# Order of the input products in the second block's mixer, with its tables and norm sums moved

## The chip, the cores and the metric

One core of a Trainium2 chip runs the whole program in one launch. The metric is the device time of an execution in microseconds (us); the kernel before took 3211.77 us (median of 3 runs, 3209.35 to 3212.21). TensorE (PE) does the matrix products and its weight loads (PEld), VectorE (DVE), ScalarE (ACT) and GpSimd (POOL) the elementwise work; SyncE (SP) and POOL issue the transfers.

## The reference

Three residual layers on x of 256 tokens by 2048 features. The first block has two (attention, then a gated linear recurrence, each with a swiglu). The second block, which the change touches, is:

```python
ada = silu(c) @ w_ada + b_ada                      # sh_m, sc_m, gt_m, sh_f, sc_f, gt_f
h = rmsnorm(x, g_pre_mix) * (1 + sc_m) + sh_m
proj = h @ w_in                                    # q (16 heads of 64), k, v (2 heads), u (1024)
attn = sliding_window_attention(q, k, v, sinks)    # window 128, softmax with a sink
y = s5_ssm(u, ...)                                 # complex diagonal state space, 64 groups of 16
z = gelu(y);  ssm = z * sigmoid(z @ w_glu)
merged = concat(rmsnorm(attn, g_attn), rmsnorm(ssm, g_ssm))
x = x + (1 + gt_m) * rmsnorm(merged @ w_out, g_post_mix)
h = rmsnorm(x, g_pre_ffn) * (1 + sc_f) + sh_f
up = causal_conv(h @ w_up);  x = x + (1 + gt_f) * rmsnorm((gelu(gate) * val) @ w_down, g_post_ffn)
```

## The kernel before

Every large product runs in three parts of split float32: the weight tile and the activations are each a high and a low part (`wh`, `wl`; two halves of `hx`), and high*high, high*low and low*high are added in PSUM. A weight tile (512 KB, tile `wr`) is loaded by SP, cast to `wh` by ACT (line 278) and subtracted to `wl` by DVE (line 97), up to two tiles ahead of its use. `gemm` and `gemm_t` walk the list of weight tiles that `plan_weights` has written; after each tile they call `tick()`, which moves every spawned generator (a "task") on to its next `yield`. So a task's yields say after how many weight tiles its next piece is traced.

That traced order is not the order on the chip. When the kernel is built, a planner puts the instructions of each engine in order by its own estimates of their durations, the traced order being the priority; weight splits and some evacuations carry a higher one (`high_priority(offset=200)`). Tiles come from pools: 56 slots of 2 KB per partition ("s"), 2 double PSUM banks for the large products (`pg`), and 4 single PSUM banks ("pa") that all small products share. On each engine the planned order is then fixed, and an instruction that isn't ready holds those behind it.

The second block's mixer (`mixer2`, from line 1232) begins at about 2123 us of the trace. Its input product `w_in` has nine column blocks of 256: block 4 with 5 (k, v and the first four query heads), 6 to 8 (the other query heads), 0 to 3 (u). Before, they run as 4, 6, 7, 8, 0, 1, 2, 3, each four weight tiles. Each query block spawns two `swa` tasks (line 1351): after two yields one head each tick (scores `psc`, softmax with Exp), later the transposes `pst`, then the values `pso`, the copies `at`, `ac` and a sum of squares. Each u block calls `utask`, which evacuates u and makes a copy `u4` by sixteen 32-partition copies on ACT (line 1245), and spawns an `ssm` task (line 1250): after one yield 32 narrow products `psz` (64 columns), then a rotation on DVE and POOL, two scans, a second rotation, and for each half the products `psy`, a Gelu (`zf`) and its split `zc`. Exp and Gelu are in different activation tables; `act` (line 115) traces a table load where the function isn't in the set that is loaded, and ties the activations of a set behind its load and the next load behind them.

An `ssm` task needs seven slots of tables (`rC`, `rS`, `rD`, four `bt`), which POOL's queue loads with 19 transfers from DRAM, where an earlier task wrote them. Before, all four sets are traced right behind the block 4 product.

After the input products come the attention half of the output product (`out2a`, four column blocks j), the four `glu` products, and the state-space half (`out2b`). `stat_rs` sums squares over the partitions by 12 products of 2 columns (`psn`) and turns the sum into 1/rms on DVE; for the state-space norm it is run by `rs_task`, two ticks into `out2b`. The rows that scale the next normalization (`d_gpf`, `d_ggf`) are made by `make_row` (line 1204: a transpose `psw`, a copy on ACT, a store by POOL), before `mixer2` begins.

Of the kernel before, what the change touches and what calls it, by code (L numbers as in the profile page):

```python
# [44 lines left out]
def ktiles(k0, k1, nkt=NKT):  # L45
    n = k1 - k0
    cnt = -(-n // nkt)
    out, a = [], k0
    for i in range(cnt):
        b = k0 + (n * (i + 1) + cnt - 1) // cnt  # L50
        out.append((a, b))
        a = b
    return out


class Build:
# [120 lines left out]

    LOAD_AHEAD, SPLIT_AHEAD, KEPT = 4, 2, 4

    def plan_weights(self):  # L180
        A = self.A
        S = []

        def add(key, aps, k0, k1, width=256, kept=0):
            seq = []
            tiles = ktiles(k0, k1, 1024 // width)
            K = []
            for i, (a, b) in enumerate(tiles):
                for bi, ap in enumerate(aps):
                    e = (ap[:, a:b, :], b - a, width, i >= len(tiles) - kept)  # L190
                    (K if e[3] else S).append(e)
                    seq.append((bi, a, b))

            for i, e in enumerate(K):
                S.insert(len(S) - 2 * (len(K) - i) + 1, e)
            self.plan.append((key, len(aps), seq))

        def out_gemm(key, w, k0, k1, kept=0):
            for j in range(4):
                add((key, j), [w[j]], k0, k1, 512, kept if j == 3 else 0)  # L200

        def ffn(l):
            for h in range(2):
                for b in self.FFN_BLOCKS[h]:
                    add(("g", l, b), [A[f"wg{l}"][b]], 0, 16, 512)
                    add(("u", l, b), [A[f"wu{l}"][b]], 0, 16, 512)
                out_gemm(("d", l, h), A[f"wd{l}"], 24 * h, (24, 44)[h], self.KEPT if l and h else 0)

        self.plan = []
        for b in (0, 1, 2, 3, 5, 4):  # L210
            add(("qkv", b), [A["wqkv"][b]], 0, 16, 512)

        seq = [(bi, a, a + 2) for r in (range(0, 12, 2), range(12, 16, 2)) for bi in range(2) for a in r]
        S.extend((A["wo"][bi][:, a:b, :], 2, 512, False) for bi, a, b in seq)
        self.plan.append((("wo", 0), 2, seq))
        for j in (2, 3):
            add(("wo", j), [A["wo"][j]], 0, 16, 512)
        ffn(0)
        for n in range(8):
            add(("xb", n), [A["wrin"][n]], 0, 16)  # L220
        for o, i in self.RNN_ORDER:
            if o == "g":
                add(("gt", i), [A["wgt"][i]], 0, 8)
            elif o == "y":
                add(("yb", i), [A["wrin"][8 + i]], 0, 16)
        out_gemm("wrout", A["wrout"], 0, 16)
        ffn(1)
        add(("in2", 4), [A["win2"][4], A["win2"][5]], 0, 16)
        for b in (6, 7, 8, 0, 1, 2, 3):
            add(("in2", b), [A["win2"][b]], 0, 16)  # L230
        out_gemm("out2a", A["wout2"], 0, 8)
        for b in range(4):
            add(("glu", b), [A["wglu"][b]], 0, 8)
        out_gemm("out2b", A["wout2"], 8, 16, self.KEPT)
        first = True
        for h in range(2):
            for b in range(11 * h, 11 * h + 11):
                if first:
                    add(("ug2", b), [A["wup2"][b], A["wup2"][22 + b]], 0, 16)
                    first = False  # L240
                else:
                    add(("u2", b), [A["wup2"][b]], 0, 16)
                    add(("g2", b), [A["wup2"][22 + b]], 0, 16)
            out_gemm(("d2", h), A["wdn2"], 22 * h, 22 * h + 22, self.KEPT if h else 0)
        self.S = S
        self.wt, self.kept = {}, []
        self.n_load = self.n_split = self.n_use = 0
        self.split_on = ["av"]
# [978 lines left out]
        self.stt(o, self.ada[:, 16 * i:16 * i + 16], 1.0, self.vec(g), ADD, MUL)  # L1227
        return o

    def mixer2(self, hx, first, rest, d_gg, d_gp):  # L1230
        nc = self.nc
        u, u4 = [None] * 4, [None] * 4

        def utask(n, ps):
            t = self.slot("ut")
            nc.scalar.copy(out=t, in_=ps[:, :, 256:512])
            o = u[n] = self.slot("u", (128, 2, 4, 64))
            for m in range(2):
                v = "p (k i) -> p i k"
                self.tt(o[:, m], ps[:, m, 0:256].rearrange(v, i=4), t[:, m, :].rearrange(v, i=4), ADD)  # L1240

            w = u4[n] = self.slot("u4", (128, 2, 4, 64))
            for lag in range(4):
                for g in range(4):
                    nc.scalar.copy(out=w[32 * lag:32 * lag + 32, :, g, :], in_=o[32 * g:32 * g + 32, :, lag, :])
# [3 lines left out]

        def ssm(q):  # L1250
            R, bt = tabs[q]
            yield
            C, S, D0 = R
            a, b, c, d = (self.slot(n, (128, 8, 64)) for n in "abcd")
            psz = [self.bank("psz").rearrange("p (j k) -> p j k", j=8) for _ in range(2)]
# [60 lines left out]
        self.spawn(rest(), False)  # L1316
        ps, psq = self.gemm(("in2", 4), hx)
        tabs = []
        for q in range(4):
            R = [self.slot(n, (128, 8, 64)) for n in ("rC", "rS", "rD")]  # L1320
            for i in range(3):
                nc.gpsimd.dma_start(out=R[i].rearrange("p a b -> p (a b)"),
                                    in_=self.d_rt[i, :, 512 * q:512 * q + 512])
            bt = {}
            for i in range(2):
                t = [self.slot("bt", (128, 4, 128)) for _ in range(2)]
                for cc in range(2):
                    bt[cc, i] = t[cc]
                    for lag in range(4):
                        nc.gpsimd.dma_start(out=t[cc][32 * lag:32 * lag + 32], in_=self.d_bt[i, lag, :, 2 * q + cc, :]  # L1330
                                            .rearrange("(g r) n -> r g n", g=4))
            tabs.append((R, bt))
        kv = self.evac(ps, "kv")
        k2, v2 = kv[:, 0, :], kv[:, 1, :]
        VP = []
# [70 lines left out]
            yield  # L1406

        ats = []
        for b in range(4):
            if b:  # L1410
                psq, = self.gemm(("in2", 5 + b), hx)
            q = self.evac(psq, "q2")
            for m in range(2):
                ats.append(self.spawn(swa(2 * b + m, q[:, m, :])))
        sts = []
        for n in range(4):
            ps, = self.gemm(("in2", n), hx)
            utask(n, ps)
            sts.append(self.spawn(ssm(n)))
        self.finish(vt, *ats)  # L1420
        self.stat_rs(sta)

# [1 line left out]
        for j in range(4):  # L1424
            ps = self.gemm_t(("out2a", j), ac)
# [22 lines left out]
        for b in range(4):  # L1448
            ps, = self.gemm(("glu", b), zc)
# [11 lines left out]
        hx = [None] * 16  # L1461
        scaled, first, rest = self.modulated(st, rows, self.ada[:, 48:64], hx)
# [8 lines left out]
            scaled(0, t)  # L1471

        def rs_task():
            yield
            yield
            self.stat_rs(sts_)

        strs = self.spawn(rs_task())
        for j in range(3):
            ps = self.gemm_t(("out2b", j), sc, 8)  # L1480
# [2 lines left out]
            for t in range(2):  # L1483
                one(j, t, ps[:, t, :])
        self.gemm_t(("out2b", 3), sc, 8, half)
        return hx, first, rest

    def post(self, mix, st, t, st2=None):

# [77 lines left out]
    def main(self):  # L1567
# [50 lines left out]
        d_ggm = self.make_row("d_ggm", self.gated("gg_m", "g_post_mix", 2))  # L1618
        self.pace = 0.45
        ada = self.spawn(self.paced(self.ada_task(72, 96)), False)  # L1620
        ssm = self.spawn(self.ssm_task())
        st2 = self.tstat()
        rows = {}
        hx = [None] * 16
        scaled, first, rest = self.modulated(st2, rows, self.ada[:, 0:16], hx)
# [9 lines left out]

        self.ffn(1, xc, st, strs, None, st2, None, half)
        self.finish(ssm, ada)
        d_gpf = self.make_row("d_gpf", self.gated("gp_f", "g_pre_ffn", 4))
        d_ggf = self.make_row("d_ggf", self.gated("gg_f", "g_post_ffn", 5))
        hx, first, rest = self.mixer2(hx, first, rest, d_ggm, d_gpf)  # L1640
        self.ffn2(hx, first, rest, d_ggf)


# [120 lines left out]
```

## Time and profile before

| | |
|---|---|
| median of 3 runs | 3211.77 us |
| the profiled execution | 3212.04 us, span of its instructions 3210.3 us |
| granted TensorE clock, mean | 0.988 of full |
| PE busy | 3128.8 us, 97% of the span |
| DVE, ACT, POOL busy | 2210.5, 1588.5, 543.9 us |
| HBM | 218 GB/s over the span |

Busy time is the union of an engine's instructions. A wait is idle time of an engine ahead of an instruction, put down to what released it. The granted clock of a stretch is 1.00 at 2.4 GHz and 0.50 at 1.2 GHz.

### The profile page before, as it was taken

Reading aid. Unit: us, or ns where it says so; the run is one execution under the profiler, and the core shown is the slowest. Engines: PE = TensorE matmul, PEld = TensorE weight load, DVE = VectorE, ACT = ScalarE, POOL = GpSimd, SP = SyncE. Lnnn points to the kernel's source line nnn. Section 1 sums busy time; section 2 is a strip of 40 time slices with the busy share of each in tenths; the row PEclk is TensorE's granted clock in tenths of the full one; section 3 lists DMA queues with packets and bytes.
Section 4 is the critical chain, followed back from the end, with each engine's and each line's share of the span. In section 5 each row is a group of like instructions: output and inputs, shape, how many; then the busy total and the mean of one; then the engine's idle time right before and its main releaser. Section 6 shows DMA issues by size and latency. Waiting matters only on the chain. (4 is left out here: it accounts for less than half of the span.)

```text
span 3210.3 us, 43992 instructions
## 1 busy us (share of the span) xinstructions
PE 3128.8 (97%) x16104; PEld 2632.9 (82%) x16104; DVE 2210.5 (69%) x3336; ACT 1588.5 (49%) x2294; POOL 543.9 (17%) x755
## 2 busy tenths in 40 slices
PE   8999999999999989999999999999998999999998
PEld 6888888888888878788887888878886888888887
DVE  7766777767777899666676667556657766456665
ACT  5554444344444477544443444447455555445553
POOL 1000000000000043087352624232211000000000
PEclk9999999999999999999999999999898999999999
DMA  7447888988887644677777777675454555655564
GB/s 264 138 142 240 283 279 282 314 269 281 278 279 263 235 145 156 189 247 253 248 258 238 241 245 247 214 220 149 141 173 148 189 188 189 196 189 188 201 192 163
DMA packets 232009, 702.54 MB, mean 219 GB/s; under 512 B 27248, under 2 KB 35504, under 8 KB 231536
## 3 DMA queue, kind: packets, MB, share of 16 engines
q1 hardware_dynamic: 221136, 671.11, 64.1%
q0 software_dynamic: 9936, 27.57, 2.7%
q8 instruction: 126, 2.06, 0.3%
q10 hardware_dynamic: 720, 1.06, 0.1%
q14 instruction: 91, 0.75, 0.1%
HBM read 683.86 MB, written 15.76 MB: 218 GB/s over the span
## 5 line engine op out<-in xcount | busy, mean ns | idle before, releaser
L97 DVE TENSOR_TENSOR wl<-wr,wh 128x1024 fp32r<-128x1024 f32 x1072 | 1352.7, 1266 | 725.9 <-ACT wh L278 646.3
L278 ACT CAST wh<-wr 128x1024 fp32r<-128x1024 f32 x1028 | 1081.6, 1052 | 1377.3 <-PE pg L143 1161.5
L143 PE MATMUL pg<-wh,xc 128*128 128x512 f32 x3200 | 802.6, 392 | 7.4 <-ACT wh L278 7.4
L143 PEld LDWEIGHTS pg<-wh,xc 128*128 128x128 f32 x3200 | 597.7, 188 | 129.8 <-ACT wh L278 7.4
L143 PE MATMUL pg<-wh,hc 128*128 128x512 f32 x2200 | 548.7, 391 | 0.0
L143 PEld LDWEIGHTS pg<-wh,hc 128*128 128x128 f32 x2200 | 410.3, 188 | 84.2
L143 PE MATMUL pg<-hh,wh 128*128 128x512 f32 x1696 | 431.3, 395 | 2.1 <-DVE kv L97 2.1
L143 PE MATMUL pg<-wl,xc 128*128 128x512 f32 x1600 | 430.1, 390 | 1.5 <-DVE wl L97 1.5
L956 DVE SCALAR_TENSOR_TENSOR aw<-aw,cb 128x512 f32<-128x512 f32 x384 | 280.9, 745 | 109.0 <-DMA aw<-in_wada 103.5
L143 PEld LDWEIGHTS pg<-hh,wh 128*128 128x128 f32 x1696 | 306.1, 190 | 60.1 <-issue 4.6
L143 PEld LDWEIGHTS pg<-wl,xc 128*128 128x128 f32 x1600 | 300.3, 188 | 64.6 <-DVE wl L97 2.4
L143 PE MATMUL pg<-wl,hc 128*128 128x512 f32 x1100 | 295.5, 390 | 5.5 <-DVE wl L97 5.4
L143 PEld LDWEIGHTS pg<-wl,hc 128*128 128x128 f32 x1100 | 205.8, 188 | 50.2 <-DVE wl L97 7.6
L143 PEld LDWEIGHTS pg<-hh,wl 128*128 128x128 f32 x1696 | 231.3, 190 | 16.8 <-issue 0.3
L143 PE MATMUL pg<-hh,wl 128*128 128x256 f32 x1696 | 237.7, 283 | 0.0
L97 POOL TENSOR_TENSOR i<-i,xv 128x512 f32<-128x512 f32 x16 | 30.3, 1895 | 962.5 <-ACT i L124 962.5
L143 PE MATMUL pg<-xc,wh 128*128 128x512 f32 x512 | 128.9, 394 | 6.0 <-DVE wh L284 5.0
L143 PEld LDWEIGHTS pg<-xc,wh 128*128 128x128 f32 x512 | 92.1, 189 | 23.6 <-DVE wh L284 5.8
L1219 POOL DMA_DIRECT2D row<-d_ggf x4 | 2.2, 547 | 566.0 <-PE pg L143 542.7
L143 PEld LDWEIGHTS pg<-xc,wl 128*128 128x128 f32 x512 | 69.8, 192 | 13.4 <-DVE wl L97 9.2
L143 PE MATMUL pg<-xc,wl 128*128 128x256 f32 x512 | 73.1, 286 | 5.6 <-DVE wl L97 5.5
L106 DVE SCALAR_TENSOR_TENSOR cv<-xpad,vecs,cv 128x256 f32<-128x256 f32 x176 | 73.4, 479 | 0.0
(328 smaller groups left out, 2831.7 us busy)
## 6 DMA issues: line engine op xcount, KB each, us to landing
aw<-in_wada SPq DMA_DIRECT2D x384, 256.0 KB, 4.7
wr<-in_wg SPq DMA_DIRECT2D x176, 512.0 KB, 4.0
wr<-in_wu SPq DMA_DIRECT2D x176, 512.0 KB, 4.0
wr<-in_wd SPq DMA_DIRECT2D x176, 512.0 KB, 4.5
wr<-in_wup SPq DMA_DIRECT2D x176, 512.0 KB, 4.7
wr<-in_wdn SPq DMA_DIRECT2D x88, 512.0 KB, 3.6
wr<-in_wrin SPq DMA_DIRECT2D x64, 512.0 KB, 4.7
wr<-in_wqkv SPq DMA_DIRECT2D x47, 512.0 KB, 3.5
```

The costliest lines, as they stand in the source:

```text
L97: return (eng or self.nc.vector).tensor_tensor(out=out, in0=a, in1=b, op=op)
L106: return self.nc.vector.scalar_tensor_tensor(out=out, in0=a, scalar=s, in1=b, op0=op0, op1=op1)
L143: self.nc.tensor.matmul(out, lhsT, rhs, start=start, stop=stop, **kw)
L278: c = self.nc.scalar.copy(out=wh[:, :n, :], in_=wr[:, :n, :])
L956: nc.vector.scalar_tensor_tensor(out=t, in0=t, scalar=1.0, in1=cb[i % 4], op0=MUL, op1=MUL, accum_out=part[:, i // 4, i % 4:i % 4 + 1])
L1219: self.nc.gpsimd.dma_start(out=t, in_=d[4 * j:4 * j + 4, :].rearrange("(o a) b -> o (a b)", o=1) .to_broadcast([128, 512]))
```

## The change

The query blocks and the u blocks are taken in turn (6, 0, 7, 1, 8, 2, 3), in the list of weight tiles and in `mixer2`. Each set of state-space tables is traced by a function `tables(q)` at four places: 0 behind the block 4 product, 1 and 2 behind query blocks 6 and 7, 3 behind u block 1. An `ssm` task yields twice, not once, ahead of `psz`. The two `make_row` calls for the norm rows move from before `mixer2` to behind `tables(0)`. `rs_task` yields four times, not twice.

```diff
+    IN2_ORDER = (6, 0, 7, 1, 8, 2, 3)
...
-        for b in (6, 7, 8, 0, 1, 2, 3):
+        for b in self.IN2_ORDER:
             add(("in2", b), [A["win2"][b]], 0, 16)
...
-    def mixer2(self, hx, first, rest, d_gg, d_gp):
+    def mixer2(self, hx, first, rest, d_gg):
...
         def ssm(q):
             R, bt = tabs[q]
-            yield
+            for _ in range(2):
+                yield
             C, S, D0 = R
...
         tabs = []
-        for q in range(4):
+
+        def tables(q):
             R = [self.slot(n, (128, 8, 64)) for n in ("rC", "rS", "rD")]
...
             tabs.append((R, bt))
+
+        tables(0)
+        d_gp = self.make_row("d_gpf", self.gated("gp_f", "g_pre_ffn", 4))
+        d_ggf = self.make_row("d_ggf", self.gated("gg_f", "g_post_ffn", 5))
...
         ats = []
-        for b in range(4):
-            if b:
-                psq, = self.gemm(("in2", 5 + b), hx)
-            q = self.evac(psq, "q2")
+        sts = []
+
+        def heads(b, ps):
+            q = self.evac(ps, "q2")
             for m in range(2):
                 ats.append(self.spawn(swa(2 * b + m, q[:, m, :])))
-        sts = []
-        for n in range(4):
-            ps, = self.gemm(("in2", n), hx)
-            utask(n, ps)
-            sts.append(self.spawn(ssm(n)))
+
+        heads(0, psq)
+        for b in self.IN2_ORDER:
+            ps, = self.gemm(("in2", b), hx)
+            if b > 4:
+                heads(b - 5, ps)
+                if b < 8:
+                    tables(b - 5)
+                continue
+            utask(b, ps)
+            sts.append(self.spawn(ssm(b)))
+            if b == 1:
+                tables(3)
         self.finish(vt, *ats)
         self.stat_rs(sta)
...
         def rs_task():
-            yield
-            yield
+            for _ in range(4):
+                yield
             self.stat_rs(sts_)
...
-        d_gpf = self.make_row("d_gpf", self.gated("gp_f", "g_pre_ffn", 4))
-        d_ggf = self.make_row("d_ggf", self.gated("gg_f", "g_post_ffn", 5))
-        hx, first, rest = self.mixer2(hx, first, rest, d_ggm, d_gpf)
+        hx, first, rest, d_ggf = self.mixer2(hx, first, rest, d_ggm)
         self.ffn2(hx, first, rest, d_ggf)
```

## Rows read from the trace of the kernel before

**Rows 1.** The page's head and first part: busy us, share, instructions of an engine.
```profile
span 3210.3 us, 43992 instructions
PE 3128.8 (97%) x16104; PEld 2632.9 (82%) x16104; DVE 2210.5 (69%) x3336; ACT 1588.5 (49%) x2294; POOL 543.9 (17%) x755
```

**Rows 2.** Waits of PE, whole span: us in total, times, longest us.
```profile
...
PE psz L143 <- ACT u L1245: 3.0, 3, 2.0
PE psn L143 <- ACT sq L120: 2.3, 1, 2.3
PE pg L143 <- DVE kv L97: 2.1, 1, 2.1
PE psz L143 <- ACT sPT L1389: 1.5, 1, 1.5
...
```

**Rows 3.** Windows: length, busy us (instructions) by engine, granted clock, DMA share, GB/s.
```profile
...
2156.78:2188.45 31.67, 29.53 (x167) 24.74 (x167) 20.12 (x59) 17.61 (x44) 18.75 (x35) 1.00 0.94 252
...
2245.31:2256.77 11.46, 11.46 (x49) 10.71 (x50) 5.66 (x7) 3.38 (x7) 2.53 (x2) 0.55 0.15 46
...
2272.19:2283.55 11.36, 11.36 (x105) 11.00 (x105) 5.96 (x7) 0.85 (x3) 2.49 (x2) 0.70 0.23 72
...
2308.30:2330.34 22.04, 21.22 (x214) 18.90 (x214) 16.88 (x29) 9.62 (x24) 5.28 (x5) 1.00 0.61 189
...
2410.41:2425.00 14.59, 14.59 (x56) 12.25 (x57) 10.58 (x23) 8.29 (x15) 1.98 (x1) 0.78 0.57 187
...
```

**Rows 4.** Timeline of PE: start, us, engine, line, operation, out<-in, count, idle before.
```profile
...
2158.92 2.06 PE L143 MATMUL pg<-hh,wh 128*128 128x512 f32 x8 [2.14 <-DVE kv L97]
...
2245.31 6.28 PE L143 MATMUL psz<-u,bt 128*128 128x64 f32 x32 [1.47 <-ACT sPT L1389]
...
2272.19 6.07 PE L143 MATMUL psz<-u,bt 128*128 128x64 f32 x32 [1.95 <-ACT u L1245]
...
2295.06 1.71 PE L143 MATMUL psz<-u,bt 128*128 128x64 f32 x12 [0.21 <-ACT u L1245]
...
2320.21 3.98 PE L143 MATMUL psz<-u,bt 128*128 128x64 f32 x32 [0.82 <-ACT u L1245]
...
```

**Rows 5.** Timeline of ACT ahead of the first `psz` and behind it.
```profile
...
2243.84 0.91 ACT L1245 COPY u<-u 32x128 f32<-32x128 f32 x3
...
2244.77 1.24 ACT L1389 COPY sPT<-pst 128x384 f32<-128x384 f32 x3
...
2246.04 1.28 ACT L135 ACT_TABLE_LOAD   x1
2247.33 0.48 ACT L1389 COPY sPT<-pst 128x384 f32<-128x384 f32 x1
...
```

**Rows 6.** Groups of ACT's instructions, 2120 to 2430: count, busy us, mean ns.
```profile
...
L1245 ACT COPY u<-u 32x128 f32<-32x128 f32 x64 | 18.9, 296 | 5.6 <-DVE u L97 4.7
...
```

**Rows 7.** Timeline of all engines around the state-space norm's sums.
```profile
...
2406.98 1.17 PE L143 MATMUL pg<-wh,sc 128*128 128x512 f32 x4
...
2409.69 1.13 ACT L120 ACTIVATE sq<-gl 128x256 f32<-128x256 f32 x2
...
2410.41 0.59 PE L143 MATMUL psn<-ones,sq 128*128 128x2 f32 x2 [2.25 <-ACT sq L120]
2410.62 1.21 ACT L120 ACTIVATE sc<-gl,vecs 128x256 fp32r<-128x256 f32 x2
...
2411.36 1.27 DVE L106 SCALAR_TENSOR_TENSOR sc<-gl,vecs,sc 128x256 fp32r<-128x256 f32 x2 [0.32 <-ACT sc L120]
...
```

**Rows 8.** Timeline of PE at the mixer's beginning.
```profile
...
2124.87 0.28 PE L1207 MATMUL psw<-ct,gg_f 128*16 128x128 f32 x1 [0.23 <-DVE xt L97]
...
2128.50 1.09 PE L1187 MATMUL psx<-ct,y 128*128 128x128 f32 x4 [3.35 <-DVE y L106]
...
```

**Rows 9.** Timeline of POOL: the first and the last of its table transfers.
```profile
...
2127.18 0.58 POOL L1322 DMA_DIRECT2D rC<-d_rt  x1
...
2190.50 0.55 POOL L1330 DMA_DIRECT2D bt<-d_bt  x1 [0.35 <-DMA bt<-d_bt]
...
```

More of the change, by code (lines that the diff above doesn't have):

```diff
@@ L1485, in mixer2 @@
         self.gemm_t(("out2b", 3), sc, 8, half)
-        return hx, first, rest
+        return hx, first, rest, d_ggf
     def post(self, mix, st, t, st2=None):
```

## The prediction, as put on record

> **What bounds the kernel now.** Read the page's head first: PE works 3128.8 of 3210.3 us, DVE 69%, ACT 49% [rows 1]. The products themselves aren't changed, so the kernel can only win what PE loses: idle time, and time at the lower of its two clocks. The second view is PE's waits. Those that the change can reach are small: three on the `u` copies, 3.0 us, one on an `sPT` copy, 1.5 us, and one on the norm's squares, 2.3 us; the 2.1 us on `kv` stands at a place that the change leaves as it is [rows 2]. The third view is the granted clock by windows, and it shows a loss that no list of waits has: behind the first `psz` group PE has 0.55, behind the second 0.70, behind the late norm sums 0.78, and 1.00 in the stretches beside them [rows 3]. 1.00 is 2.4 GHz and 0.50 is 1.2 GHz, so a window's length times what it lacks to 1.00 is the loss: 11.46 x 0.45 = 5.2 us, 11.36 x 0.30 = 3.4 us, 14.59 x 0.22 = 3.2 us. The fourth view, PE's timeline, shows what went before. A wait of 1.47 and one of 1.95 us ahead of 32 narrow products were followed by the low clock; waits of 0.21 and 0.82 us ahead of the same products were not, nor was 2.14 us ahead of full-width ones [rows 4].
>
> So at stake are, for the four `psz` groups, 1.47 + 5.2 + 1.95 + 3.4 + 0.21 + 0.82 = 13.0 us, and for the norm sums 2.25 + 3.2 = 5.4 us [rows 3, 4, 7]: 18.4 us, 0.6% of the span. Nothing else that is slow lies in reach.
>
> **Part 1, the order.** No instruction is added to PE, DVE or POOL; what moves is when they come due. Counting yields: before, the first `psz` is traced in the tick of the last heads' transposes `pst`, and its wait ends on the copy `sPT` of such a transpose, which sits on ACT right behind the last three `u4` copies [rows 4, 5]. The four "pa" banks explain that: `psz` takes two, one still held by a `pst`. After, with two yields, the `psz` of u blocks 0, 1, 2 fall in ticks 10, 18, 26 behind the block 4 product, where the running heads trace nothing (scores in ticks 6, 7, 14, 15, 22, 23, transposes in 9, 17, 25, values in 11, 19, 27). That clash goes.
>
> What is late next is ACT. Sixteen copies at 0.296 us are 4.7 us [rows 6], and casts come between; the second to fourth `psz` all waited for them, by 1.95, 0.21 and 0.82 us [rows 2, 4], though the planner had put other products first. Its estimate is short, and the extra yield doesn't mend that, since a `psz` that isn't ready by plan is planned later anyway. Three of four copy chains now run beside softmaxes. The price per `psz` lies between 0.21 us (third) and 1.47 + 5.2 = 6.6 us (first). I take one of the four at 6.0 us, the mean of the two that lost the clock, and three at 0.5 us, the mean of the two that didn't: 7.5 us, a gain of 13.0 - 7.5 = 5.5 us. The ends are four at 0.21 (gain 12.2) and four at 6.6 (loss 13.4).
>
> **Part 2, activation tables.** Before, all Exp of the heads come ahead of all Gelu of the state space, and one load of 1.28 us lies between [rows 5]. After, by the same count of yields, Gelu falls in ticks 15, 18, 23, 26 and Exp in 14, 15, 22, 23: the set changes seven times, six more, 6 x 1.28 = 7.7 us of ACT. ACT is busy 17.6 of 31.7 us with heads in flight [rows 3], so most of that hides in its idle time; the load in tick 18 stands inside the copy chain of u block 1 (spawned at tick 16). I charge one load, 1.3 us; ends 0 and 7.7 us. The ties between sets also force an order: the second Exp of query block 2 behind the first Gelu of u block 0, which waits for its `psy`. By the traced order that `psy` lies seven ticks behind its u block, and nothing but the heads' own later steps waits for that Exp, so I give it no price of its own.
>
> **Part 3, tables as needed.** The same 76 transfers. Before they ran on POOL from 2127.2 to 2191.1 us [rows 9] beside full DMA traffic (share 0.94) with PE at clock 1.00 and no PE wait on a transfer [rows 2, 3]. Spread out they can collide with POOL's two products of each rotation, which come behind them on its queue: 64 us for four sets is 16 us each. Sets 1, 2 and 3 are traced in ticks 4, 12 and 16 and read by `psz` in ticks 18, 26 and 30; 14 ticks of more than 2 us each [rows 4] cover 16 us, so the data is in time, and slots are free for longer. I take 0; ends -1 us (a slot comes sooner) and +4 us (a rotation behind transfers, cover gone).
>
> **Part 4, norm rows.** Two transposes `psw` go from an idle stretch of 3.35 us on PE [rows 8], where they cost nothing, to the first product. There they take 2 x 0.28 = 0.6 us unless they fall in the `kv` wait [rows 4]. Their two copies on ACT and two stores on POOL are small and wait for nothing. The row that ends the 3.35 us is DVE's `y`, so removing them does not shorten it. I take +0.3 us; ends 0 and 0.6.
>
> **Part 5, norm sums later.** `psn` now stands behind the fourth weight tile of `out2b`, not the second, so PE doesn't meet the late square. But the fourth tile needs the `sc` made of the same `glu` output. From 2406.98 us, the third tile's 12 products at about 0.25 us [rows 4] end near 2409.9; the first high half of `sc` is there at 2410.62 + 0.6 = 2411.2, its low half at 2411.36 + 0.64 = 2412.0 [rows 7]. PE waits 1.3 + 0.6 = about 2 us, as long as before: the wait changes its name. What can be won is the clock, because full-width products follow now instead of 2-column ones; the 2.14 us ahead of full-width products kept it [rows 4]. Half of 3.2: gain 1.6 us. Ends: 3.2, and -2 us if the norm's DVE chain, now shorter by two tiles of cover, holds up the bank that column block 2 needs.
>
> **Sum.** 5.5 - 1.3 - 0 - 0.3 + 1.6 = 5.5 us faster. The profiled execution took 3212.04 us, 1.7 us more than its span and 0.3 us over the median: 3212.0 - 5.5 = 3206.5, and by the median 3206.3. I forecast **3206 us**.
>
> **Rivals.** (A) Every wait becomes as short as the fourth `psz` (0.82 us) and the clock holds throughout: 13.0 - 4 x 0.82 = 9.7, plus 3.2, plus nothing lost to tables: 12.9 us, **3199 us**. For it: the bank clash goes and narrow groups lie among wide products; against it: two of three waits on the copies weren't due to the clash. (B) The losses move and stay: the two expensive `psz` lose 6 us again under other names and the norm's wait goes to `sc` with the low clock behind it: **3211 us**. For it speaks that an ACT behind its plan caused most waits; against it that one cause of two at `psz` is gone. (C) Slower: the loads of activation tables decide. Those in ticks 18 and 26 stand in the copy chains of u blocks 1 and 2 and push them from 1.7 us (mean of the two long waits) to 1.7 + 1.28 = 3.0 us, beyond the length from which the low clock followed (1.47 us; 0.82 us didn't); each then costs 3.0 + 4.3 = 7.3 us. With the first at 6.6 and the last at 0.8 that is 22.0 against 13.0, and 0.3 for the transposes: +9.3 us, **3221 us**. For it: six loads certain; against: ACT has 14 us idle in 31.7 [rows 3]. The Trainium skill speaks for it too: "ScalarE: Activation LUTs", section "Table sets: the hidden batching unit" wants functions grouped by set, and its section "What ACT_TABLE_LOAD costs" puts a switch at about 2.66 us with the drain. The trace bears out only the load: 1.28 us, the next copy 0.01 us behind it [rows 5]; by the page six switches would be an estimated 16 us of ACT. That the change doesn't do what it says is possible for part 3 (the planner may issue the transfers as soon as slots are free, as now); the time is then the forecast's.
>
> **Numbers.** 0.2%, 6.4 us, is about what a measurement can tell from no change: below 3205.3 is faster, above 3218.2 slower. Forecast 0.44, with its own range of 3201 to 3211, half of it below 3205.3; A 0.20; B 0.22; C 0.14. Faster 0.22 + 0.20 = 0.42, same 0.22 + 0.22 = 0.44, slower 0.14. The range takes in A and most of the way to C: 3196 to 3220.
>
> **What would show it.** Right: seven table loads among heads and state space; `psz` waits on `u` copies, not on `sPT`; at most one or two windows under 0.9 between 2160 and 2330 us; no wait at `psn`, but one of some 2 us on `sc` ahead of the fourth `out2b` tile; the `psw` in the first product and PE's 3.35 us wait unchanged. Wrong: waits on `psy` or scans behind POOL's transfers, a wait of the second `out2b` pair for a `pg` bank, or a low clock behind three or four `psz`.

## The result, and the profile after

The changed kernel takes 3237.74 us (median of 4 runs, 3233.33 to 3244.71) where the kernel before takes 3211.99 beside it: 1.0082 of its time (95% interval 1.0070 to 1.0094), 26 us slower. The forecast was 3206, the range ended at 3220.

The profiled execution took 3241.56 us. Its page begins with the rows that answer to [rows 1]:

```profile
span 3239.8 us, 43999 instructions
PE 3134.5 (97%) x16104; PEld 2635.6 (81%) x16104; DVE 2212.0 (68%) x3336; ACT 1596.2 (49%) x2300; POOL 544.2 (17%) x755
```

The counts of instructions are the same but for six more on ACT, the activation table loads. Where the time went is read from windows by stage: the input product, the attention half of the output product (`out2a`) and the state-space half (`out2b`). Before:

```profile
core 0: us, PE busy (x) PEld busy (x) DVE busy (x) ACT busy (x) POOL busy (x), PEclk, DMA share, GB/s
2130.20:2308.30 178.10, 171.49 (x1100) 148.57 (x1100) 116.63 (x248) 98.94 (x235) 56.56 (x85) 0.94 0.56 160
2308.30:2379.10 70.80, 69.98 (x587) 60.83 (x587) 38.10 (x48) 30.44 (x50) 9.96 (x10) 1.00 0.55 175
2401.40:2452.10 50.70, 48.40 (x206) 39.59 (x204) 38.32 (x56) 29.92 (x52) 15.62 (x13) 0.93 0.62 208
```

After:

```profile
2133.00:2327.30 194.30, 167.68 (x1043) 143.46 (x1042) 109.33 (x241) 98.56 (x218) 48.57 (x72) 0.90 0.47 140
2327.30:2411.50 84.20, 79.53 (x644) 68.70 (x645) 45.64 (x57) 38.95 (x76) 13.26 (x12) 0.98 0.47 148
2433.80:2481.40 47.60, 45.72 (x206) 37.15 (x204) 38.13 (x57) 29.76 (x52) 15.02 (x13) 1.00 0.68 222
```

The first two stretches grew by 16.2 and 13.4 us, 29.6 together: PE's idle time in them from 7.4 to 31.3 us, its busy time from 241.5 to 247.2 (the clock). The third shrank by 3.1. PE's waits, which answer to [rows 2], name the idle time (us in total, times, longest):

```profile
PE psc L143 <- DVE q L97: 13.1, 2, 8.8
...
PE pst L1395 <- DVE sP L101: 4.9, 2, 3.5
...
PE pg L143 <- DVE col L103: 3.1, 1, 3.1
PE psy L143 <- DMA kt<-d_kt: 3.1, 1, 3.1
...
PE psz L143 <- ACT sPT L1397: 1.3, 1, 1.3
...
PE psz L143 <- ACT u L1247: 0.3, 1, 0.3
```

The waits at `psz`, about which the prediction turned, have shrunk from 4.5 to 1.6 us: the three on the `u` copies from 3.0 to 0.3, the one on `sPT` only from 1.5 to 1.3. A wait that the prediction did not have, for a query block `q`, took 13.1. The timeline shows how late the evacuation of such a block is, that is, the copy and the add that bring a product out of its PSUM banks. PE ends block 0's and block 7's products in these rows, at 2191.3 and 2209.5 us:

```profile
2190.17 1.12 PE L143 MATMUL pg<-hh,wl 128*128 128x256 f32 x8
...
2208.81 0.72 PE L143 MATMUL pg<-hh,wl 128*128 128x256 f32 x4
```

and DVE empties their banks in these, done at 2209.9 and 2233.1:

```profile
2209.26 0.59 DVE L97 TENSOR_TENSOR u<-pg,ut 128x256 f32<-128x256 f32 x1
...
2232.39 0.68 DVE L97 TENSOR_TENSOR q<-pg,q 128x512 f32<-128x512 f32 x1
```

The delays are 18.6 and 23.5 us. There are two such double banks, so wide products stop when both are full. From here on this delay is the measure (us from the end of a product to the add that frees its bank):

| block | 6 | 0 | 7 | 1 | 8 | 2 | 3 |
|---|---|---|---|---|---|---|---|
| before (order 6, 7, 8, 0, 1, 2, 3) | 6.1 | 6.0 | 3.0 | 9.1 | 3.3 | 21.9 | 7.8 |
| after | 5.8 | 18.6 | 23.5 | 32.3 | 53.5 | 44.5 | 28.2 |
| e4, tables early | 5.8 | 5.1 | 4.8 | 15.9 | 29.4 | 13.7 | 28.4 |
| e10, set 1 late | 5.8 | 18.6 | 23.8 | 15.2 | 29.1 | 13.6 | 28.4 |
| e11, set 1 late, begun at once | 5.9 | 5.1 | 12.6 | 15.2 | 29.8 | 13.7 | 28.4 |
| e8, e4 with early evacuation tiles | 2.1 | 5.1 | 5.4 | 3.6 | 3.9 | 8.4 | 27.1 |
| e12, e8 with one yield | 2.1 | 5.1 | 2.9 | 2.6 | 7.8 | 4.9 | 16.6 |

### The profile page after: what moved, and what is told of

Read it like the earlier page. It is cut to its first block, busy times and chain, and to the rows that moved or that the text cites. A ratio compares the mean times of both kernels' runs of the same rounds, so it can differ in the third digit from the quotient of the medians.

```text
span 3239.8 us, 43999 instructions
## 1 busy us (share of the span) xinstructions
PE 3134.5 (97%) x16104; PEld 2635.6 (81%) x16104; DVE 2212.0 (68%) x3336; ACT 1596.2 (49%) x2300; POOL 544.2 (17%) x755
## 5 line engine op out<-in xcount | busy, mean ns | idle before, releaser
L97 DVE TENSOR_TENSOR wl<-wr,wh 128x1024 fp32r<-128x1024 f32 (+1 forms) x1072 | 1348.3, 1262 | 743.5 <-ACT wh L280 666.6
L143 PEld LDWEIGHTS pg<-xc,wl 128*128 128x128 f32 x512 | 69.5, 191 | 13.4 <-DVE wl L97 8.8
```

Source lines behind the costliest of these rows:

```text
L97: return (eng or self.nc.vector).tensor_tensor(out=out, in0=a, in1=b, op=op)
L143: self.nc.tensor.matmul(out, lhsT, rhs, start=start, stop=stop, **kw)
```

## The experiments

Each ratio is to the kernel before, run on the same chip; 0.001 is 3.2 us.

| kernel | order, tables, yields | median us | ratio, 95% interval |
|---|---|---|---|
| after | new, late, 2 | 3237.7 | 1.0082 (1.0070 to 1.0094) |
| e1 | new, one set for all, 2 | 3220.5 | 1.0030 (1.0018 to 1.0043) |
| e2 | after, no Gelu | 3244.6 | 1.0107 (1.0092 to 1.0122) |
| e3 | old, late, 2 | 3232.0 | 1.0065 (1.0048 to 1.0082) |
| e4 | new, early, 2 | 3223.4 | 1.0038 (1.0023 to 1.0053) |
| e6 | old, early, 1 | 3212.6 | 0.9995 (0.9986 to 1.0004) |
| e7 | after, table tiles begun at once | 3234.0 | 1.0063 (1.0044 to 1.0082) |
| e8 | e4, evacuation tiles begun early | 3221.3 | 1.0018 (1.0009 to 1.0028) |
| e9 | new, early, 1 | 3222.5 | 1.0028 (1.0019 to 1.0038) |
| e10 | e4, set 1 late | 3230.8 | 1.0054 (1.0040 to 1.0068) |
| e11 | e10, table tiles begun at once | 3225.8 | 1.0040 (1.0024 to 1.0055) |
| e12 | e8 with one yield | 3213.4 | 1.0002 (0.9993 to 1.0011) |
| e13 | e7, set 2 behind block 6 | 3227.2 | 1.0043 (1.0030 to 1.0057) |
| e14 | e13 with e8's tiles and one yield | 3221.4 | 1.0027 (1.0016 to 1.0038) |
| e15 | old, early, 2 | 3210.4 | 0.9993 (0.9984 to 1.0002) |
| e16 | e12, half of the u4 copies on DVE | 3212.4 | 1.0000 (0.9991 to 1.0009) |
| e17 | e6, half of the u4 copies on DVE | 3209.8 | 0.9991 (0.9983 to 1.0000) |

### Which part costs: e1 to e4

Three theories stood first. S: more tiles are alive than the 56 slots hold. G: the ties between Exp and Gelu hold up the heads. D: the tables' transfers come late or stand in the way.

**e1**, only set 0 is loaded, and all four state-space tasks read it:

```diff
         def tables(q):
+            if q:
+                tabs.append(tabs[0])
+                return
```

> The changed kernel, but the tables of sets 1 to 3 are not loaded: all four state-space tasks read set 0 (21 slots and 57 transfers fewer; the state space is computed with the wrong tables). Theory S (slots): the new order keeps more tiles alive at once than the 56 slots hold, the copies that empty the product banks (q, ut, u) get no slot for 19 to 53 us, and PE's wide products wait for their two banks. Then the copies come within 4 us of the product, the waits at psc on q (4.3 and 8.8 us) go, and the time falls from 3238 to 3212 or below. Theory G (activation sets): Exp and Gelu in turn hold ACT's order; seven loads stay here, so it stays above 3230. Theory D (late transfers on POOL and kt): the 3.1 us wait on kt goes, 3232 to 3235.

1.0030, a time that none of the three theories gave, and the delays of blocks 0 and 7 are 5.0 and 4.5 us. Most of the loss hangs on sets 1 to 3.

**e2**, the Gelu is a plain copy, so that no table changes and no tie is left:

```diff
-                self.act(zf[q][:, cc, :], psy[:, 0:256], AF.Gelu_apprx_tanh)
+                self.act(zf[q][:, cc, :], psy[:, 0:256], AF.Identity)
```

> The changed kernel, but the state space's Gelu is replaced by Identity, which is in every activation set: no table loads and no ties between heads and state space (the Gelu is left out). G: at or below 3215. S: the tiles alive are nearly the same, so 3228 to 3238; some 3 to 8 us come off because heads no longer hold their slots while their Exp waits behind a Gelu.

No faster, 1.0107, and slower than S said too, with delays as in the changed kernel. G falls.

**e3**, the old order with all else as changed:

```diff
-    IN2_ORDER = (6, 0, 7, 1, 8, 2, 3)
+    IN2_ORDER = (6, 7, 8, 0, 1, 2, 3)
```

> The changed kernel with the old order of blocks (6, 7, 8, 0, 1, 2, 3) alone; tables as needed, two yields, norm rows and norm sums stay changed. S and G: the whole loss goes, and what is left is the gain of the late norm sums, about 3 us: 3207 to 3211. D: tables in the middle still collide, 3215 to 3230.

1.0065, nearest to what D gave: undoing the order recovers little while the tables are late.

**e4**, the new order with all four sets traced behind block 4, as before:

```diff
-        tables(0)
+        for q in range(4):
+            tables(q)
...
-                if b < 8:
-                    tables(b - 5)
...
-            if b == 1:
-                tables(3)
```

> The changed kernel, but all four table sets are traced behind the block 4 product, as before the change. S: more slots are held early, the loss stays or grows, 3237 to 3260. G: as the changed kernel, 3233 to 3242. D: the transfers no longer stand among the rotations, 3220 to 3230.

1.0038, the time that D gave, and not resolved from that of e1, though four early sets hold more slots for longer. So S falls too: late tables cost 0.0044, 14 us, and it isn't for want of slots. How lateness costs that much is still open here.

### Why late tables cost: e7, e10, e11, e13

What holds up block 7? In the changed kernel the transposes of the heads of block 6 run on PE from 2181.3 us:

```profile
2181.27 0.49 PE L1395 MATMUL pst<-ct,sP 128*128 128x128 f32 x3
...
2195.85 1.57 PE L143 MATMUL psc<-kv,q 64*128 64x128 f32 x8
```

Their copies `sPT` come on ACT only at 2194.1, with ACT idle ahead of each of the three casts in front of them (in brackets: idle time, and what ended it):

```profile
2187.14 1.05 ACT L280 CAST wh<-wr 128x1024 fp32r<-128x1024 f32 x1 [0.84 <-ACT ses L124]
2190.41 1.05 ACT L280 CAST wh<-wr 128x1024 fp32r<-128x1024 f32 x1 [2.23 <-PE pg L143]
2193.16 1.05 ACT L280 CAST wh<-wr 128x1024 fp32r<-128x1024 f32 x1 [1.70 <-PE pg L143]
2194.12 1.61 ACT L1397 COPY sPT<-pst 128x384 f32<-128x384 f32 x4
```

Four `pst` fill all four small banks until then, so the next scores `psc` wait until 2195.9. In e4 the first copies come 3.4 us behind the start of their transposes, not 12.9:

```profile
2173.41 0.49 PE L1396 MATMUL pst<-ct,sP 128*128 128x128 f32 x3
...
2176.79 0.86 ACT L1398 COPY sPT<-pst 128x384 f32<-128x384 f32 x2
```

ACT was not busy. Nor were the transfers what it lacked: POOL issued the last of set 1 before 2174.8 us, some 19 us ahead of these copies. So it is the plan. In the built program the tiles of the slot pool begin in exactly the order in which they were traced: of 1306, four are out of turn. (The 356 tiles of the small banks: none.) Here are tiles of that pool in the traced order, with the number of wide products (`hh` with a weight tile) planned ahead of the first write of each, counted from the first transfer of set 0. The first row begins with set 1, the third ahead of set 3:

```
after:  rC@147 rS@152 rD@154 bt@159 bt@175 bt@193 bt@210  sPT@210 sPT@212 sPT@212 sPT@212
e4:     (all sets done by 60)                             sPT@152 sPT@155 sPT@162 sPT@167
after:  u4@380 rC@381 rS@384 rD@388 bt@393 bt@413 bt@430 bt@444  sPT@444 ... a@444 e@444 q2@444
```

A slot is taken at a tile's first write, in turn. The seventh tile of set 1 is first written by the 16th of POOL's 19 transfers, and everything traced behind it stands in line for that, whether or not slots are free: `sPT` has the same 210 as the last `bt`. This is theory L, the slot line. It foretold that an early first write would open the line.

**e7**, every table tile is begun at once by a one-column write; the transfers keep their place in the trace:

```diff
+            B = [[self.slot("bt", (128, 4, 128)) for _ in range(2)] for _ in range(2)]
+            for t in R + B[0] + B[1]:
+                nc.vector.memset(t[:, 0, 0:1], 0.0)
```

> The changed kernel; the seven tiles of each table set are begun by a one-column write of VectorE right where the set is traced, so that their slots are taken at once; the 19 transfers stay where they are. Theory L (the slot line): slots are handed out in the traced order, a tile takes its slot when its first writer is planned, and the last tile of a set is first written by the 16th of 19 transfers that POOL issues one after another (about 0.8 us each, 13 us); every tile traced behind it (sPT, sP, at, ut, u, the next q) waits in the plan for that, set by set. L expects the delays from the end of a product to its evacuation to fall from 18.6 and 23.5 us (blocks 0 and 7) to about 5, and the time to come near the 3223 us that the kernel took with all sets traced early: 3219 to 3229. Theory S (too few slots): slots are taken earlier and for longer, so it gets no better: 3236 or more. Theory D (transfers too late, on POOL's queue or for their readers): the transfers stand where they stood: 3236 to 3240, with the waits of POOL for slots unchanged.

The time missed, 1.0063. The first half of the line opened: block 0's u is added at 2195.6 us, not 2209.3, and the plan shows why, since the last tile of set 1 is begun at 144 and not at 210:

```
e7:     rC@137 rS@138 rD@143 bt@143 bt@144 bt@144 bt@144  sPT@144 sPT@148 sPT@149 sPT@150
```

POOL issued set 1 later than in the changed kernel, from 2178.7 us and not from 2161.2 (its place in the trace is the same, its time is not), and the evacuation came earlier all the same. So it did not wait for the data of the set. But a new stall took much of the gain, at `psy`, which multiplies u by `kt`, a matrix of 256 KB that SP loads (`ca` is loaded by SP too, behind it). PE, in the first row, and SP, in the second, which issued the transfer that PE waits for:

```profile
2237.70 2.61 PE L143 MATMUL psy<-u,kt 128*128 128x256 f32 x8 [8.95 <-DMA kt<-d_kt]
```

```profile
2226.67 0.33 SPq L1289 DMA_DIRECT2D kt<-d_kt  x1
```

The transfer took 11.0 us, while POOL issued set 2 from 2225.49 to 2244.4. In the kernel before, kt lands in 2.6 to 6.9 us. So D seems to be part of the truth as well. The next three separate the two.

**e10** is e4 with set 1 alone late, behind block 6, when no kt is under way:

> The kernel with the new order and early tables (3223 us), with one set alone, set 1, traced late, behind query block 6; it is not read before u block 1's psz, some 50 us later, and no kt or ca transfer is under way then. L (the slot line): everything traced behind the set's last tile waits in the plan until POOL has issued 16 transfers, so the evacuations of blocks 0 and 7 go back to some 18 and 23 us behind their products, as in the changed kernel: 3227 to 3233. D (only late transfers that hit others cost): nothing is hit, delays of 5 us, 3221 to 3225.

Delays 18.6 and 23.8 us, 1.0054: L, and not D. Its plan has the numbers of the changed kernel, 147 to 210 for set 1 and 210 for `sPT`.

**e11** adds e7's one-column writes:

> The kernel before this one, with the seven tiles of each set begun at once by one-column writes. L: the delays of blocks 0 and 7 are back at about 5 us and the time at that of the early tables: 3221 to 3226. D: no difference between the two kernels, both at 3221 to 3225. S (too few slots): no difference between them either, both slow.

Delays 5.1 and 12.6, and the input product takes 178.4 us (182.1 in e10, 177.8 in e4): 1.0040, in the span that L gave, with block 0's delay as it said and block 7's half way. The times alone (1.0054, 1.0040, and 1.0038 of e4) have overlapping intervals; the delays decide.

**e13** is e7 with set 2 traced together with set 1:

```diff
-                if b < 8:
-                    tables(b - 5)
+                if b == 6:
+                    tables(1)
+                    tables(2)
```

> The changed kernel with its table tiles begun at once (3234 us), and set 2 traced with set 1 behind block 6, not behind block 7. In that kernel PE stood still for 8.95 us for a kt transfer that took 11 us while POOL moved set 2. D, as far as it goes: moved away from kt, set 2 lets the kt land in 3 to 6 us, the wait goes, and with the low clock behind it some 9 to 12 us: 3222 to 3226. If the collision was not the cause, the wait stays and the time at 3232 to 3236.

No kt wait is left, kt lands within 6.1 us, and the time is 1.0043, just above the span that D gave. By time e13 isn't resolved from e7, and its profiled execution (3220.8 us) was the fastest of its four. The two repairs together are: 1.0043 against 1.0082 of the changed kernel, close to the 1.0038 of early tables.

### Why the new order costs: e6, e15, e8, e9, e12

**e6** has the old order, early tables and one yield; only the norm rows and sums are moved:

> The kernel after with the old block order, all four table sets behind block 4 and one yield ahead of psz: what is left of the change is the moved norm rows (part 4) and the later norm sums (part 5). The norm sums were worth 3.1 us in the second half of the output product of the changed kernel (47.6 against 50.7 us). If the loss of the change sits in the order, the yields and the late tables alone, as both theories below say, this kernel gains that: 3208 us (3206 to 3210) beside 3211 for the kernel before, with the input product at 178 us and its banks freed after 3 to 22 us as before. If moving the rows costs something that nobody counted, it is at 3211 or above.

0.9995: 1.6 us gained, not resolved from nothing; `out2b` takes 47.6 us as in the changed kernel.

**e15** is e6 with two yields:

> Old order, early tables, norm rows and sums moved, two yields ahead of psz: all that the change does without its new order and its late tables. With one yield it took 3212.6 us (0.9995 of before). If the second yield does no harm where no heads follow it: 3210 to 3214. If it costs some 3 us also here, since every state-space task ends a tick later in the output product: 3214 to 3218, with out2a at 72 to 74 us instead of 70.7. With tables late this kernel took 1.0065; whatever it takes here, the difference is the price of late tables in the old order.

0.9993: the yield does no harm here. Against e3 it gives the price of late tables in the old order, 0.0072 or 23 us. Against e4 it gives the price of the new order: 0.0045, 14 us. By stage, in the profiled executions:

| us | input product | `out2a` | both |
|---|---|---|---|
| before | 178.1 | 70.8 | 248.9 |
| after | 194.3 | 84.2 | 278.5 |
| e15, old order, early | 180.9 | 69.5 | 250.4 |
| e3, old order, late | 176.6 | 91.5 | 268.1 |
| e4, new order, early | 177.8 | 84.5 | 262.3 |
| e12, new order, early, both repairs (below) | 172.0 | 82.0 | 254.0 |

Only the sum of both can be compared, because work moves between them. In e3 the input product is shorter because more of the state space falls behind it: two groups of `psz` run in `out2a`, in e15 one. Its plan has the slot line again, set by set, up to the tile `a` with which the second state-space task's rotation begins:

```
e3:     bt@210 sPT@210 ... bt@306 sPT@306 ... bt@500 kt@508 ca@508 ca@508 a@508
e15:    (all sets done by 60)  sPT@152 ... sPT@204 ...    kt@416 ca@420 ca@425 a@435
```

508 is the end of the input product. No run of the old order has its tables late and its tiles begun early, so there the plan is all that speaks for L.

The slot line is a candidate for the price of the order too. In e4's plan the tiles traced around block 1, whose product ends at 317 by the same count, are:

```
kt@258  sP@284 sP@300  zf@307 zc@322  sP@322 sP@357  kt@363 ca@367 ca@371  ut@380 u@380 u4@380  sPT@403
```

Four softmaxes, a Gelu and two sets of transfers of other tasks stand ahead of `ut`, and the u copies ahead of the next `sPT`. In the old order heads stand behind heads.

**e8** begins q2, or ut, u and u4, by a one-column write ahead of their product:

```diff
+            T = early(self.slot("q2")) if b > 4 else early(
+                self.slot("ut"), self.slot("u", (128, 2, 4, 64)), self.slot("u4", (128, 2, 4, 64)))
             ps, = self.gemm(("in2", b), hx)
```

> The kernel with the new order and all tables early (3223 us); the tiles that take up each product (q2, or ut, u and u4) are begun by a one-column write ahead of that product, so that they no longer queue for a slot behind the softmax tiles of the heads traced during the product. L expects that the evacuations of blocks 1 and 8, 15.9 and 29.4 us behind their products, come within about 6 us, that those of 2 and 3 (13.7 and 28.4) stay late behind the second and third rotation, and that PE's waits for q (4.1 us) and for u (3.5 us) mostly go: 3214 to 3220. A rival, O: the new order itself makes ACT and DVE late (softmax, copies u4 and rotations in each other's way, whatever the slots): then the evacuations stay late and the time stays at 3221 to 3226.

The delays of blocks 1 and 8 fell from 15.9 and 29.4 to 3.6 and 3.9 us, as L said and O did not. The time, 1.0018, lies between both and isn't resolved from e4's. Its profile has two new waits for kt:

```profile
PE psy L143 <- DMA kt<-d_kt: 8.7, 2, 4.4
```

These are not collisions: the two transfers landed in 4.8 and 3.9 us, with no table set under way. They were issued only 4.9 and 4.0 us ahead of the products that read them, and PE, whose order is fixed, waited for them.

**e9** is e4 with one yield:

> The kernel with the new order and all tables early (3223 us), with one yield ahead of psz as before the change, not two. My prediction held the second yield to be what lets the new order win, by keeping psz away from the transposes pst. If so, one yield brings the wait on sPT back and costs up to 6 us: 3225 to 3229. L: a tick earlier, each state-space task asks for its slots earlier and is done a tick earlier, so that the output product meets less unfinished work: 3216 to 3221, with the stretch of out2a at 78 to 82 us instead of 84.5.

1.0028 and 82.2 us in `out2a` instead of 84.5, against my own reading of the yield; by time alone the two kernels aren't resolved.

**e12** joins e8 and e9:

> New order, early tables, evacuation tiles begun ahead of their products and one yield ahead of psz: the two repairs that gained some 6 and 3 us by themselves. If they add up, 3212 to 3216, within 0.2% of the kernel before; input product and out2a together 250 to 255 us instead of 262. If the order has a cost of its own that neither slots nor yields explain (theory O), 3219 or more. As a try for a better kernel, the new order would have to come out under 3209, which I do not expect.

1.0002. The input product, 172.0 us, is now 6 us shorter than before, `out2a` 11 longer (82.0), with 32 `psz`, 16 `pso` and 12 `psn` more in it and 72 `psy` fewer. With slots taken early and one yield the new order costs nothing that can be measured, and this time is clear of e4's. How the gain divides between the two repairs isn't shown.

### What is left: e14, e16, e17

**e14** is e13 with e8's tiles and one yield, late tables with every repair:

> The changed kernel with every repair and the tables still as needed: table tiles and evacuation tiles begun by one-column writes, set 2 moved up behind block 6, one yield. The same kernel with early tables took 3213 us (1.0002 of before). L and D together (slots and the collision are all that late tables cost): 3213 to 3218. If late tables have a third cost, POOL's queue or the slots themselves: 3221 or more.

1.0027 against e12's 1.0002: late tables cost some 8 us more than L and the one collision explain. Its profile has four short kt waits (3.6 us in all) and 3.4 us for the rotation `a`; its profiled execution was one of the faster ones (3216.2 us, median 3221.4). What the rest is stays open.

**e16** and **e17** are e12 and e6 with eight of the sixteen u4 copies on DVE:

```diff
-                    nc.scalar.copy(out=w[32 * lag:32 * lag + 32, :, g, :], in_=o[32 * g:32 * g + 32, :, lag, :])
+                    (nc.vector.tensor_copy if g % 2 else nc.scalar.copy)(
+                        out=w[32 * lag:32 * lag + 32, :, g, :], in_=o[32 * g:32 * g + 32, :, lag, :])
```

> New order, early tables, evacuation tiles begun early, one yield (3213 us, 1.0002), with eight of the sixteen u4 copies of each u block on VectorE, eight left on ACT. In that kernel PE waits 4.3 us for the copies ahead of one psz and runs at 0.69 and 0.79 of full clock in the 20 us that follow. If the copies' time on ACT is what is left of the order's cost: 3205 to 3210. If the wait only moves to the rotation or to sPT: 3211 to 3215.

> Old order, early tables, one yield, rows and sums moved (3212.6 us, 0.9995), with eight of the sixteen u4 copies of each u block on VectorE. It waits 3.9 us for the copies and 1.5 for sPT ahead of psz, with clock windows of 0.83 to 0.92 behind them. If the copies are the cause, these waits and most of the low clock go: 3204 to 3209. If the clock falls anyway behind the narrow products: 3209 to 3212.

1.0000 and 0.9991. The wait for the copies stays (3.2 and 5.0 us in one piece), so halving their number on ACT doesn't remove it. e17 is the fastest kernel of all, by less than can be told from no change.

## Why the prediction was wrong

**Part 3, tables as needed: the step that failed most.** It said that the data is in time and "slots are free for longer", and charged 0, with ends at -1 and +4 us. Late tables cost 14 us in the new order and 23 in the old. The data was in time for `psz`; what was late is all that is traced behind a set, since slots go out in the traced order and a set takes its last slot at its 16th transfer. For the new order e10 and e11 show that by the delays, e7 by its plan and e13 by the time. A second cost, that a set's transfers fall on those of kt, rests on one stall, seen in e7 and gone in e13. The prediction did name waits "behind POOL's transfers" as a sign of being wrong; in the changed kernel that sign was 3.1 us of kt, and POOL itself stood still for 8.0 and 5.3 us inside set 3 until products `psy` of PE had ended.

**Part 1, the order: wrong in sign.** It took a gain of 5.5 us with ends at 12.2 gained and 13.4 lost. With early tables it lost 14 us. What it said of `psz` came out the other way round: the wait on `sPT`, which the second yield was to remove, stayed (1.3 of 1.5 us), and the waits on the copies, which were to stay, went (0.3 of 3.0 us). The low clock came at other places and more often. One or two windows under 0.9 were expected between 2160 and 2330 us; of nine stretches of 20 us from 2160 us on, these four are:

```profile
2220.00:2240.00 20.00, 15.69 (x79) 13.29 (x78) 15.21 (x15) 5.06 (x10) 12.55 (x15) 0.83 0.36 108
2240.00:2260.00 20.00, 16.92 (x120) 14.60 (x120) 8.91 (x26) 7.62 (x15) 6.49 (x12) 0.83 1.01 273
2260.00:2280.00 20.00, 14.72 (x83) 11.76 (x79) 6.55 (x19) 14.05 (x34) 9.21 (x17) 0.83 0.34 93
...
2300.00:2320.00 20.00, 17.23 (x125) 14.88 (x126) 9.32 (x29) 7.70 (x17) 3.24 (x3) 0.75 0.04 8
```

The step that failed is the list of what moves: it followed `psz` and the heads by their ticks and left out who queues for slots between them, above all the evacuations, which hold the two wide banks. e8 shows it by the delays, and the time came back in e12, with the second yield gone as well. That yield, half of the argument, is worth nothing in the old order and costs perhaps 3 us (e4 to e9) to 5 us (e8 to e12) in the new one, neither resolved.

**Part 2, activation tables: count right, charge too high.** Seven loads of 1.28 us came, the first and the last here:

```profile
2253.41 1.28 ACT L135 ACT_TABLE_LOAD   x1
...
2324.08 1.28 ACT L135 ACT_TABLE_LOAD   x1
```

Without them (e2) the kernel is no faster. Rival C came nearest to the time, 3221 (17 us short), and by luck: its mechanism played no part. It was the one for which the Trainium skill spoke ("ScalarE: Activation LUTs", section "Table sets: the hidden batching unit", which wants functions grouped by set); the grouping counted for nothing that a run resolves here. That ACT's idle time took up the loads is likely (it is busy 98.6 of the 194.3 us of the input product) but not shown by itself.

**Part 4, norm rows: right in the rows, too small to time.** Both `psw` fall in the first product, at the `kv` wait (2.4 us, before 2.1), and PE's wait for `y` ahead of it stayed:

```profile
2131.40 0.66 PE L1189 MATMUL psx<-ct,y 128*128 128x128 f32 x4 [3.92 <-DVE y L106]
...
2159.28 0.27 PE L1209 MATMUL psw<-ct,gp_f 128*16 128x128 f32 x1
2159.38 0.27 PE L1209 MATMUL psw<-ct,gg_f 128*16 128x128 f32 x1
```

**Part 5, norm sums later: right in the rows.** The wait moved from `psn` to `sc`, 1.66 + 0.23 us where "about 2" was said, and full-width products behind it kept the clock, 1.00 where [rows 3] has 0.78:

```profile
2443.84 0.51 PE L143 MATMUL pg<-wh,sc 128*128 128x512 f32 x1 [1.66 <-ACT sc L120]
2444.57 1.89 PE L143 MATMUL pg<-wh,sc 128*128 128x512 f32 x7 [0.23 <-DVE sc L106]
```

That is 3.1 us of `out2b` in the profiled execution against the 1.6 taken, at the upper end; e6, which times parts 4 and 5, has a gain of 1.6 us (-1.3 to 4.5) where 1.3 was taken, and so doesn't resolve it.

**The range** ended at 3220, short of rival C, whose price too was counted in waits at `psz`. The first step of the prediction counted what PE loses now and said that nothing else lies in reach; a wait that the kernel before doesn't have, like the 13.1 us for `q`, had hardly a place in it. No row of the kernel before shows what a later-traced tile holds up, and I took that silence for a price of 0.

## What to carry to other kernels

Where a planner hands out a pool's buffers in the traced order, what is traced late to save buffers holds up everything traced behind it until its last tile is first written; look for idle engines whose next instruction only lacks a buffer, and begin such tiles early or give the loads a pool of their own (the latter was not tried). Before tasks of two kinds are traced in turn, list the tiles that each asks for: a short evacuation queues behind the slowest task ahead of it. And follow the buffers that free the bottleneck's banks first, not the waits that are largest now.

## What the runs showed of the hardware

A 256 KB transfer issued by SP took 11.0 us to land (e7) while POOL had a table set's 19 transfers under way; the eight of its kind took 2.6 to 6.9 us in the kernel before, where no table set moves beside them. During the slow one PE was busy 2.1 of 11.0 us, and the mean DMA share was 0.93:

```profile
2226.67:2237.70 11.03, 2.08 (x12) 1.45 (x11) 3.69 (x15) 2.77 (x10) 4.97 (x10) 0.77 0.93 233
```

The Trainium skill says it in general ("DMA: Bandwidth & Descriptors", section "Issuing engines are not separate DMA queues"): what different engines issue shares the same 16 DMA engines. This trace agrees: the kt transfer was issued by SP, the set by POOL, and with the two moved apart no kt took more than 6.1 us (e13). But a table set isn't needed for a slow one. In e3 a kt took 8.8 us from 2353.0 us, with no table set under way and a DMA share of 0.99, while PE stayed busy:

```profile
2353.00:2362.00 9.00, 9.00 (x94) 7.97 (x93) 3.92 (x5) 3.18 (x6) 0.67 (x2) 1.00 0.99 287
```

Both slow landings fell on busy DMA engines, whoever had filled them; how much of the 11.0 us was due to the set and how much to the weight tiles beside it isn't shown.
